# Order of the first loads and place of the bias tables in a hybrid sparse-attention decoder step

## The chip, the cores and the metric

The kernel runs on one core of a Trainium2 chip. The metric is device time in microseconds (us) of one execution. The core has five engines, each with an instruction queue of its own that is worked off in order: TensorE (PE in the profile; its weight loads are listed apart as PEld), VectorE (DVE), ScalarE (ACT), GpSimd (POOL) and SyncE (SP), which here issues nearly all DMA transfers. TensorE runs at one of two clocks, 1.2 or 2.4 GHz.

## What is computed

One layer of a decoder, for a prompt of 512 tokens and 8 sample tokens that share the weights. The part that matters here is the head of the layer: an adaLN modulation of the input by a condition vector, then the input projections. All logits of the attention branches get a bias that depends on the distance alone, from a table of 32 buckets by 16 heads.

```python
shift, scale, gate = jnp.split(jax.nn.silu(c) @ w_ada + b_ada, 3, axis=-1)
h = x * (1.0 + scale[:, None, :]) + shift[:, None, :]
parts = jnp.split(h @ w_in, np.cumsum(IN_WIDTHS)[:-1], axis=-1)
...
bias_c = tab_g[:, t5_bucket(dist_c), :].transpose(1, 0, 3, 2)
s_c = jnp.einsum('bqgrd,bngd->bqgrn', qc, ck) * scale + bias_c
```

Behind it come three attention branches (compressed, selected, window), a block-sparse branch, gates, projections and a LayerNorm. The change does not touch these.

## The kernel before

A scheduler places the instructions of each engine; the code gives dependences, priorities by the order of writing, and a few explicit orders.

The width of 1024 is cut into 8 tiles of 128 channels. For each tile `j`, `load_ada(j)` fetches two pieces of the adaLN weights (`u<-ada_ss`, 128x1024 f32 each, so 1.05 MB a tile), `load_x(j)` the tile's rows of the transposed x (128x520). `ada(j)` multiplies the weights with the condition (`s<-u,cs`, 8 matmuls into one bank of the two called `s`), ACT copies the result to `a`, two small matmuls (`s<-cst,a`) turn it into columns, DVE adds the bias (`ssh`), and ACT and DVE form h of this tile as a high and a low part (`hTh`, `hTl`). `ada(j)` also asks for the loads of tile `j + 3`. The weights of two successive tiles share one buffer `u`, and there are two such buffers: the loads of tiles 4 and 5 wait until TensorE has read tiles 0 and 1, those of 6 and 7 until it has read 2 and 3.

Three projections of h (columns `kc`, `vc`, `ks`) are worked as the tiles come: `early_load` fetches a column block of weights (`raw<-w_cols`, 128x1024) and splits it in high and low parts on ACT, DVE and POOL (`v`, `kd`, `kl`), and `early_mm(n, k)` adds tile `k` to the sums with 6 matmuls 128x260 for each of the three, 18 a tile and 144 in all, into the banks `d`, `d`, `d`, `o`, `e`, `pt`.

`tables()` makes the bias tables from two inputs, `tabx` (33x272) and `e` (33x3010), which lie in the buffer `y`: one matmul 16x384, 15 matmuls 128x8, and two of 128x194 and 128x130, each block into a bank that DVE then copies out (`bs`, `bc`, `bdn`, `bdm`). Before the change these use the one bank `e`. `bs` is written out to DRAM much later, for the attention.

Behind the last tile, TensorE goes on with the other projections (`d<-hTh,hl`), merged with the compression network and then with the attention. Their weights come through SP's queue behind the loads of the start, in the order of the code; an SP load waits, too, until the load eight places ahead of it has landed. Behind the adaLN loads stand small ones: `pt16` (from which DVE computes `vidx`) and `pos`.

Of the kernel before, what the change touches and what calls it, by code (L numbers as in the profile page):

```python
# [190 lines left out]
def build(tc, A):  # L191
    nc = tc.nc
# [4 lines left out]
    def mm(out, lhsT, rhs, start, stop):  # L197
        if glue[1] is None:
            i = mmraw(out, lhsT, rhs, start=start, stop=stop, skip_group_check=True)  # L199
        else:  # L200
            with tc.high_priority():
                i = mmraw(out, lhsT, rhs, start=start, stop=stop, skip_group_check=True)  # L202
            order(i, glue[1])
        if glue[0]:
            glue[1] = i
        return i
# [19 lines left out]
    def lo(out, x, hi, eng=None):  # L226

        if eng is None:
            eng = engs[0][turns[0] % len(engs[0])]
            turns[0] += 1  # L230
        (nc.gpsimd if eng == "p" else nc.vector).tensor_sub(out, x, f32(hi))  # L231
# [4 lines left out]
    with ExitStack() as es:  # L236
# [10 lines left out]
        def bank(tag, bufs):  # L247
            return ps.tile([128, 512], F32, name=tag, tag=tag, bufs=bufs)

        def p_d():  # L250
            return bank("d", 3)

        def p_s():
            return bank("s", 2)
# [7 lines left out]
        def p_e():  # L262
            return bank("e", 1)

        def row(tag, bufs=1):
            return kvp.tile([128, NT], F32, name=tag, tag=tag, bufs=bufs)

        def pair(tag, dtype):
            return kvp.tile([128, 2, NT], dtype, name=tag, tag=tag, bufs={"kd": 3, "v2": 2}[tag])
# [78 lines left out]
        def expect(n):  # L348
            got = next(at_w)
            assert got == n, (got, n)  # L350
# [42 lines left out]
        e, tabx = y2[:33, 0:NE], y2[:33, NE:NE + 272]  # L393
# [15 lines left out]
        def load_x(j):  # L409
            if j < 8:  # L410
                if j < 4:
                    xr[j] = row(*(("ev", 2), ("z", 1), ("tmp", 1), ("ev", 2))[j])
                else:
                    xr[j] = st.tile([128, NT], F32, name="xr", bufs=4)
                nc.sync.dma_start(xr[j], A["xT"][j])
# [6 lines left out]
        def load_ada(j):  # L422
            if j >= 8 or j in ss:
                return
            if j % 2 == 0:
                ss["t"] = u_tile(F32)
            ss[j] = ss["t"][:, j % 2]
            for hf in range(2):
                c = slice(hf * 1024, hf * 1024 + 1024)
                ss["dma"] = nc.sync.dma_start(ss[j][:, c], A["ada_ss"][j][:, c])  # L430

        def ada(j):

            p = p_s()
            for hf in range(2):
                for k in range(4):
                    c = hf * 1024 + k * 256
                    mm(p[32 * k:32 * k + 32, :256], cs[:, hf * 4 + k], ss[j][:, c:c + 256], hf == 0, hf == 1)
            load_x(j + 3)
            load_ada(j + 3)  # L440
            a = st.tile([128, 256], F32, name="a", bufs=2)
            nc.scalar.copy(a, p[:, :256])
            for i in range(2):
                D["seli"] = mm(p[:, 256 + i * 16:266 + i * 16], a[:, 128 - i * 128:256 - i * 128], const("seli"), True, True)
            nc.vector.tensor_add(ssh[:, j], view(p, 256, [[16, 2], [1, 10]]), view(bT, j, [[8, 2], [0, 10]]))
            x = xr.pop(j)
            h = st.tile([128, NT], F32, name="h")
            sh, s1 = (ssh[:, j, i] for i in range(2))
            D["act"] = nc.scalar.activation(hTh[:, j, :T], x[:, :T], AF.Identity, scale=s1[:, 0:1], bias=sh[:, 0:1])
            nc.vector.tensor_mul(h[:, T:], x[:, T:], s1[:, 1:9])  # L450
            nc.vector.tensor_add(h[:, T:], h[:, T:], sh[:, 1:9])
            nc.vector.tensor_copy(hTh[:, j, T:], h[:, T:])
            nc.vector.tensor_scalar(h[:, :T], x[:, :T], s1[:, 0:1], sh[:, 0:1], op0=OP.mult, op1=OP.add)
            D["dve"] = nc.vector.tensor_sub(hTl[:, j], h, f32(hTh[:, j]))
# [3 lines left out]
        def tables():  # L458

            nc.gpsimd.memset(bc[:, :, 0:16], 0.0)  # L460
            nc.gpsimd.memset(bc[:, :, 31:64], BIG)
            nc.gpsimd.memset(cv2, 0.0)
            nc.gpsimd.memset(zn, 0.0)
            p = p_e()
            mm(p[:16, :384], tabx[:, 0:16], e[:, E_BAND:E_CMP], True, True)
            bs = st.tile([16, 384], F32, name="bs")
            nc.vector.tensor_copy(bs, p[:16, :384])
            D["band"] = bs
            p = p_e()
            for m in range(15):  # L470
                mm(p[:, m * 8:m * 8 + 8], e[:, E_CMP + m * 128:E_CMP + m * 128 + 128], tabx[:, 0:8], True, True)
            nc.vector.tensor_copy(bc[:, :, 16:31], p[:, :120].rearrange("p (m h) -> p h m", h=8))
            p = p_e()
            mm(p[:, :194], tabx[:, 16:144], e[:, E_DEC:E_WIN], True, True)
            mm(p[:, 256:386], tabx[:, 144:272], e[:, E_DEC:E_DEC + 130], True, True)
            nc.vector.tensor_copy(bdn, p[:, :194])
            nc.vector.tensor_copy(bdm, p[:, 256:386])
# [3 lines left out]
        def early_load(n):  # L481

            expect(n)
            raw = W.take(0)
            early_w[n] = []
            for hf in range(2):
                if n == "ks" and hf:
                    t = [kvp.tile([128, T], F32R, name="kl", tag="kl", bufs=2) for _ in range(2)]
                else:
                    t = pair("v2" if n == "kc" else "kd", F32R)  # L490
                    t = [t[:, x, :512] for x in range(2)]
                nc.scalar.copy(t[0], HALVES[hf](raw))
                lo(t[1], HALVES[hf](raw), t[0])
                early_w[n].append(t)

        def early_mm(n, k):
            if k == SELI_K:
                with tc.issue_after(D["seli"].ins):
                    return early_mms(n, k)
            early_mms(n, k)  # L500
# [9 lines left out]

        EARLY = "kc", "vc", "ks"
        nc.sync.dma_start(cT, A["cT"])
        nc.sync.dma_start(tabx, A["tabx"])
        nc.sync.dma_start(e, A["e"])
        load_ada(0)
        nc.sync.dma_start(cst0, A["cst"][:, :NC0])
        nc.sync.dma_start(bT, A["bT"])
# [8 lines left out]
        for j in range(3):  # L526
            if j:
                load_ada(j)
                load_x(j)
            early_load(EARLY[j])  # L530
        for j in range(9):
            if j < 8:
                ada(j)
            if j == 1:
                tables()
            if j:
                for n in EARLY:
                    early_mm(n, j - 1)
# [1035 lines left out]
        p = p_d()  # L1574
# [4 lines left out]
        for tt in range(4):  # L1579
            next(few, None)  # L1580
            c = 0
            for n in PARTS[tt]:
                p = p_d()[:, :n]
# [111 lines left out]
```

## Time and profile before

| | |
|---|---|
| timed runs | 657.27, 663.61, 663.81 us; median 663.61 us |
| the profiled execution | 660.91 us, of which the span in the trace is 659.1 us |
| mean granted TensorE clock in it | 0.974 |
| busy: PE, DVE, ACT, POOL | 619.0 (94%), 310.5, 295.2, 287.3 us |
| DMA | 124.77 MB, mean 189 GB/s |

A row of a timeline gives the start of a group of like instructions, how long it lasts, the engine, line, operation and what is read and written (output <- inputs), the count, and in brackets how long the engine sat idle ahead of it and what ended that. The matmuls of `s<-u,cs`, `s<-cst,a` and `e<-y` count twice in the timeline, since they run in two passes (a row of x16 `s<-u,cs` is the 8 matmuls of a tile); those of 128x260 count once. The ends of matmuls are modelled, so the start of the next row tells better how long a group took. A granted clock of 1.00 stands in rows of the windows ahead of the first change of clock that was recorded, whatever the clock was.

### The profile page before, as it was taken

Reading aid. Unit: us, or ns where it says so; the run is one execution under the profiler, and the core shown is the slowest. Engines: PE = TensorE matmul, PEld = TensorE weight load, DVE = VectorE, ACT = ScalarE, POOL = GpSimd, SP = SyncE. Lnnn points to the kernel's source line nnn. Section 1 sums busy time; section 2 is a strip of 40 time slices with the busy share of each in tenths; the row PEclk is TensorE's granted clock in tenths of the full one; section 3 lists DMA queues with packets and bytes.
Section 4 is the critical chain, followed back from the end, with each engine's and each line's share of the span. In section 5 each row is a group of like instructions: output and inputs, shape, how many; then the busy total and the mean of one; then the engine's idle time right before and its main releaser. Section 6 shows DMA issues by size and latency. Waiting matters only on the chain.

```text
span 659.1 us, 13320 instructions
## 1 busy us (share of the span) xinstructions
PE 619.0 (94%) x4747; PEld 518.1 (79%) x4747; DVE 310.5 (47%) x800; ACT 295.2 (45%) x679; POOL 287.3 (44%) x328
## 2 busy tenths in 40 slices
PE   6999999999979799999999899998988999999993
PEld 4778999999959578776879679865635998999672
DVE  1465543532572664335355446744431145545177
ACT  2248455544443545444445446645433353433521
POOL 1105466542352433442364544445432264655746
PEclk9998999999998969999999989999998999999998
DMA  8895554539953594699775563168977344345102
GB/s 309 337 293 188 167 179 144 171 98 97 165 186 104 155 360 141 216 310 311 245 229 196 196 237 97 49 220 312 304 264 288 100 153 137 96 129 188 68 24 106
DMA packets 64132, 124.77 MB, mean 189 GB/s; under 512 B 8142, under 2 KB 28368, under 8 KB 63521
## 3 DMA queue, kind: packets, MB, share of 16 engines
q1 hardware_dynamic: 61954, 116.58, 52.9%
q0 software_dynamic: 2112, 7.34, 6.3%
q8 instruction: 37, 0.61, 0.4%
q14 instruction: 29, 0.24, 0.1%
HBM read 112.76 MB, written 11.13 MB: 188 GB/s over the span
## 4 chain that ended last, share of the span: by engine, by line
PE 66%; DMA 6%; SPq 3%; DVE 3%; issue 2%; ACT 1%; POOL 1%; POOLq 0%; ACTq 0%; DVEq 0%
PE d L199 40%; PE s L199 9%; PE e L199 7%; DMA raw<-mobv 3%; PE pt L1025 3%; SPq L721 2%; PE o L202 2%; PE o L199 2%; PE pt L199 1%; PE e L202 1%; DMA raw<-slcv,vidx 1%; DMA raw<-winv 1%; DVE xt L1488 1%; DMA craw<-cmp 1%; SPq L717 0%
## 5 line engine op out<-in xcount | busy, mean ns | idle before, releaser
L199 PE MATMUL d<-hTh,hl 128*128 128x260 f32 (+1 forms) x1408 | 273.1, 290 | 1.4 <-DVE hl L231 1.1
L199 PEld LDWEIGHTS d<-hTh,hl 128*128 128x128 f32 (+1 forms) x1408 | 221.4, 189 | 16.8 <-issue 9.4
L199 PE MATMUL d<-hTl,hl 128*128 128x260 f32 (+1 forms) x704 | 201.4, 287 | 0.0
L199 PEld LDWEIGHTS d<-hTl,hl 128*128 128x128 f32 (+1 forms) x704 | 133.2, 189 | 3.2 <-issue 2.5
L231 POOL TENSOR_TENSOR hl<-raw,hl 128x512 fp32r<-128x512 f32 x56 | 73.5, 1314 | 104.2 <-ACT hl L310 99.6
L310 ACT CAST hl<-raw 128x512 fp32r<-128x512 f32 (+1 forms) x111 | 67.8, 615 | 76.1 <-PE d L199 62.6
L1018 POOL TENSOR_SCALAR p<-p,sm,gp 128x512 f32<-128x512 f32 (+1 forms) x64 | 40.0, 626 | 95.8 <-DVE sm L1017 91.2
L1016 ACT ACTIVATE p<-s,sm 128x512 f32<-128x512 f32 (+1 forms) x96 | 50.8, 530 | 65.9 <-PE pt L1025 54.0
L231 DVE TENSOR_TENSOR hl<-raw,hl 128x512 fp32r<-128x512 f32 (+1 forms) x55 | 53.5, 974 | 49.4 <-ACT hl L310 47.6
L199 PE MATMUL d<-yh,hl 128*128 128x260 f32 x256 | 46.3, 282 | 0.0
L1025 PE MATMUL pt<-cst,p 128*128 128x128 f32 x240 | 40.3, 282 | 1.5 <-DVE pp L1030 0.8
L199 PEld LDWEIGHTS d<-yh,hl 128*128 128x128 f32 x256 | 39.7, 188 | 1.0 <-issue 0.4
L199 PE MATMUL s<-kd,q 128*128 128x512 f32 (+1 forms) x96 | 35.1, 366 | 4.6 <-ACT p L1016 4.6
L1010 DVE TENSOR_REDUCE sm<-s 128x1 f32<-128x256 f32 (+1 forms) x48 | 16.9, 354 | 44.9 <-PE s L199 43.9
L1025 PEld LDWEIGHTS pt<-cst,p 128*128 128x128 f32 x240 | 27.8, 142 | 11.5 <-issue 5.8
L1018 POOL TENSOR_SCALAR p<-p,sm,cst 128x512 f32<-128x512 f32 (+3 forms) x32 | 19.5, 611 | 38.1 <-DVE sm L1017 37.9
L199 PE MATMUL d<-yl,hl 128*128 128x260 f32 x128 | 36.0, 282 | 0.0
L199 PE MATMUL s<-u,w1h 128*128 128x256 f32 (+1 forms) x160 | 33.5, 301 | 1.2 <-ACT u L793 0.7
L1012 DVE CUSTOM_DVE_ANT_0 s<-s,band 128x256 f32<-128x256 f32 (+1 forms) x48 | 17.3, 362 | 35.2 <-PE s L199 24.8
L199 PEld LDWEIGHTS s<-kd,q 128*128 128x128 f32 x96 | 18.6, 194 | 17.8 <-ACT p L1016 8.6
L231 POOL TENSOR_TENSOR u<-craw,u 128x512 fp32r<-128x512 f32 x16 | 21.3, 1331 | 24.8 <-ACT u L828 24.8
L199 PE MATMUL s<-kd,qx 128*128 128x512 f32 (+1 forms) x96 | 31.5, 330 | 0.0
(425 smaller groups left out, 1167.3 us busy)
## 6 DMA issues: line engine op xcount, KB each, us to landing
raw<-w_cols SPq DMA_DIRECT2D x46, 512.0 KB
raw<-mobk SPq DMA_DIRECT2D x64, 256.0 KB
raw<-mobv SPq DMA_DIRECT2D x64, 256.0 KB
u<-ada_ss SPq DMA_DIRECT2D x16, 512.0 KB
craw<-cmp SPq DMA_DIRECT2D x64, 128.0 KB
raw<-slck SPq DMA_DIRECT2D x64, 64.0 KB
raw<-ada_g SPq DMA_DIRECT2D x8, 512.0 KB
raw<-w_up SPq DMA_DIRECT2D x8, 512.0 KB
```

Of the source, the lines that this page charges most:

```text
L199: i = mmraw(out, lhsT, rhs, start=start, stop=stop, skip_group_check=True)
L202: i = mmraw(out, lhsT, rhs, start=start, stop=stop, skip_group_check=True)
L231: (nc.gpsimd if eng == "p" else nc.vector).tensor_sub(out, x, f32(hi))
L310: nc.scalar.copy(h, src)
L721: dyn.append(nc.sync.dma_start(out, A[name][bass.ds(page, 1)].rearrange("a p c -> p (a c)")))
L1010: nc.vector.tensor_reduce(sm[:, 0:1], s[:, :b], axis=AX, op=OP.min)
L1012: nc.vector.tensor_tensor_reduce(out=s[:, b:n], in0=s[:, b:n], in1=j.band[:, 256 - (n - b):], scale=1.0, scalar=top, op0=OP.add, op1=OP.mi ...
L1016: nc.scalar.activation(pr, s[:, :n], AF.Exp, scale=-1.0, bias=sm[:, 1:2], accum_out=sm[:, 2:3])
L1018: nc.gpsimd.tensor_scalar(pr, pr, sm[:, 3:4], j.gate(i), op0=OP.mult, op1=OP.mult)
L1025: nc.tensor.transpose(p[:, k * 128:k * 128 + 128], j.p[i][:, kb * 128:kb * 128 + 128], ident)
L1488: add(xt[tt][:, c], xt[tt][:, c], u)
```

## The change

The loads of `tabx` and `e` are issued behind those of adaLN tile 1 and its rows of x, and no longer ahead of tile 0. `tables()` is written behind `ada(3)`, and no longer behind `ada(1)`. Its three blocks take a bank of the pair `s`, which the adaLN tiles use as well, in place of the bank `e`.

```diff
-            p = p_e()
+            p = p_s()
             mm(p[:16, :384], tabx[:, 0:16], e[:, E_BAND:E_CMP], True, True)
...
-            p = p_e()
+            p = p_s()
             for m in range(15):
...
-            p = p_e()
+            p = p_s()
             mm(p[:, :194], tabx[:, 16:144], e[:, E_DEC:E_WIN], True, True)
...
         nc.sync.dma_start(cT, A["cT"])
-        nc.sync.dma_start(tabx, A["tabx"])
-        nc.sync.dma_start(e, A["e"])
         load_ada(0)
...
             if j:
                 load_ada(j)
                 load_x(j)
+            if j == 1:
+                nc.sync.dma_start(tabx, A["tabx"])
+                nc.sync.dma_start(e, A["e"])
             early_load(EARLY[j])
         for j in range(9):
             if j < 8:
                 ada(j)
-            if j == 1:
+            if j == 3:
                 tables()
```

TensorE's queue from its first matmul on, before. The tables are `e<-y`, the adaLN tiles 0 and 1 `s<-u,cs`:

```order
L199 MATMUL e<-y 16x384
L199 MATMUL s<-u,cs 32x256 x4
L199 MATMUL e<-y 128x8 x10
L199 MATMUL s<-u,cs 32x256 x4
L199 MATMUL e<-y 128x8 x5
L199 MATMUL s<-u,cs 32x256 x8
L199 MATMUL s<-cst_72,a 128x10 x2
L199 MATMUL e<-y 128x194
L199 MATMUL e<-y 128x130
L199 MATMUL s<-cst_72,a 128x10 x2
L199 MATMUL s<-u,cs 32x256 x8
L199 MATMUL d<-hTh,v_136 128x260 x4
```

The same place after; `v` holds the weights of `kc`, `kd` here those of `vc`:

```order
L199 MATMUL s<-u,cs 32x256 x8
L199 MATMUL s<-cst_72,a 128x10 x2
L199 MATMUL s<-u,cs 32x256 x4
L199 MATMUL d<-hTh,v_134 128x260 x4
L199 MATMUL d<-hTl,v_134 128x260 x2
L199 MATMUL s<-u,cs 32x256 x4
L199 MATMUL s<-cst_72,a 128x10 x2
L199 MATMUL d<-hTh,kd 128x260
L199 MATMUL o<-hTh,kd 128x260
L199 MATMUL s<-u,cs 32x256 x4
L199 MATMUL d<-hTh,kd 128x260
```

The tables are gone from here, and the first early projections stand between the halves of adaLN tile 1 and ahead of tile 2, where before they stood behind tile 2.

The place in TensorE's queue to which the tables went (`s<-y`), after; ahead of its first row stand the second half of adaLN tile 3 and the columns of tile 2, and the row of `s<-cst` here is the columns of tile 3:

```order
L199 MATMUL s<-y 16x384
L199 MATMUL d<-hTh,v_134 128x260 x2
L199 MATMUL d<-hTh,kd 128x260 x2
L199 MATMUL e<-hTh,kd 128x260 x2
L199 MATMUL d<-hTh,v_134 128x260 x2
L199 MATMUL o<-hTh,kd 128x260 x2
L199 MATMUL pt<-hTh,kd 128x260 x2
L199 MATMUL s<-cst_72,a 128x10 x2
L199 MATMUL s<-y 128x8 x15
L199 MATMUL s<-y 128x194
L199 MATMUL s<-y 128x130
L199 MATMUL d<-hTl,v_134 128x260 x2
```

All of the tables now stand behind adaLN tile 3, in the midst of the early projections for tile 2.

VectorE's queue behind the tables' first copy, after; `h<-xr` is tile 4's h:

```order
L472 COPY bc<-s 128x8x15
L476 COPY bdn<-s 128x194
L477 COPY bdm<-s 128x130
L445 TENSOR_TENSOR ssh<-s,bT 128x20
L543 TENSOR_SCALAR vidx<-pt_107,cst_72 128x8
L450 TENSOR_TENSOR h<-xr,ssh 128x8
L453 TENSOR_SCALAR h<-xr,ssh 128x512
```

`vidx`, which needs the load of `pt16`, stands ahead of the h of tile 4 here; before, it stood behind that of tile 5.

## Rows read from the trace of the kernel before

**Rows 1.** The page: the chain that ended last, shares of the span by engine.

```profile
PE 66%; DMA 6%; SPq 3%; DVE 3%; issue 2%; ACT 1%; POOL 1%; POOLq 0%; ACTq 0%; DVEq 0%
```

**Rows 2.** Timeline of TensorE, 6.5 to 24 us: start, length, what, idle time ahead.

```profile
6.54 1.44 PE L199 MATMUL e<-y 33*16 33x384 f32 x2 [6.54 <-DMA y<-e]
7.91 1.08 PE L199 MATMUL s<-u,cs 128*32 128x256 f32 x8
8.92 4.43 PE L199 MATMUL e<-y 33*128 33x8 f32 x20
13.28 1.08 PE L199 MATMUL s<-u,cs 128*32 128x256 f32 x8
14.29 2.30 PE L199 MATMUL e<-y 33*128 33x8 f32 x10
16.52 1.93 PE L199 MATMUL s<-u,cs 128*32 128x256 f32 x16
18.39 1.03 PE L199 MATMUL s<-cst,a 128*128 128x10 f32 x4
19.34 1.44 PE L199 MATMUL e<-y 33*128 33x194 f32 x4
20.72 1.02 PE L199 MATMUL s<-cst,a 128*128 128x10 f32 x4
21.67 1.93 PE L199 MATMUL s<-u,cs 128*32 128x256 f32 x16
23.53 1.24 PE L199 MATMUL d<-hTh,v 128*128 128x260 f32 x4
```

**Rows 3.** The same timeline from 24 us to the end of the start.

```profile
24.57 0.64 PE L199 MATMUL d<-hTh,kd 128*128 128x260 f32 x2
25.00 0.64 PE L199 MATMUL o<-hTh,kd 128*128 128x260 f32 x2
...
27.82 0.33 PE L199 MATMUL pt<-hTh,kd 128*128 128x260 f32 x1
27.98 0.40 PE L199 MATMUL d<-hTl,v 128*128 128x260 f32 x2
...
30.43 1.07 PE L199 MATMUL s<-u,cs 128*32 128x256 f32 x16
...
34.45 0.51 PE L199 MATMUL s<-cst,a 128*128 128x10 f32 x4
34.89 1.50 PE L199 MATMUL s<-u,cs 128*32 128x256 f32 x24
...
40.89 0.40 PE L199 MATMUL d<-hTh,kd 128*128 128x260 f32 x2
41.13 0.41 PE L199 MATMUL e<-hTh,kl 128*128 128x260 f32 x2
...
52.37 0.51 PE L199 MATMUL d<-hTh,hl 128*128 128x260 f32 x2
```

**Rows 4.** DMA view of 0 to 70 us: GB/s in 40 slices of 1.75 us.

```profile
GB/s 0 120 268 329 360 417 409 408 419 405 415 420 398 394 403 413 389 68 75 323 344 300 303 139 283 194 358 398 332 337 257 168 307 171 0 0 157 205 254 150
```

**Rows 5.** Timeline of ScalarE: splits of the first two weight blocks, and `pos`.

```profile
11.01 1.14 ACT L492 CAST v<-raw 128x512 fp32r<-128x512 f32 x2 [8.14 <-DMA raw<-w_cols]
...
15.48 1.14 ACT L492 CAST kd<-raw 128x512 fp32r<-128x512 f32 x2 [0.68 <-DMA raw<-w_cols]
...
41.27 0.21 ACT L784 CAST u<-pos 128x16 fp32r<-128x16 f32 x1 [0.16 <-DMA pos<-pos]
```

**Rows 6.** Timeline of TensorE at 60 us: narrow matmuls of the compression network.

```profile
60.38 0.39 PE L199 MATMUL s<-u,w1h 128*128 128x66 f32 x2
...
61.95 0.36 PE L199 MATMUL s<-u,w1h 128*128 128x66 f32 x1 [0.68 <-ACT u L793]
```

**Rows 7.** Windows of 1 us: us, busy of PE, PEld, DVE, ACT, POOL, granted clock, DMA.

```profile
61.00:62.00 1.00, 0.32 (x3) 0.08 (x2) 0.72 (x2) 0.96 (x3) 0.23 (x1) 1.00 0.00 0
62.00:63.00 1.00, 1.00 (x6) 0.91 (x6) 0.93 (x4) 0.98 (x3) 0.00 (x0) 0.52 0.00 0
...
65.00:66.00 1.00, 1.00 (x9) 0.86 (x7) 0.00 (x0) 0.00 (x0) 0.52 (x1) 0.77 0.83 234
```

## The prediction

> **What bounds the kernel now.** The page's chain of waits comes first: matmuls on TensorE make up two thirds of it, and DMA 6% [rows 1]. Nothing in the body waits for a fixed time; transfers run at 189 GB/s in the mean, where the start shows over 400 [rows 4]. So what the start takes less, the end takes less, and the edit is judged by one number: when TensorE turns from the early projections to the first `d<-hTh,hl`, before at 52.37 us [rows 3].
>
> TensorE's own timeline comes next. It starts at 6.54, when `e` has landed, and from there on its rows follow each other almost without a hole up to 52.37 [rows 2, 3]. That it is the bound of the start, and not the loads, is seen at adaLN tile 2: TensorE comes to it at 21.67, and its 5.28 MB of loads had passed by 17.0 (below).
>
> The second thing to see there is the clock. Rows of 128x260 start 0.43 us apart for two at 24.57 and 25.00, which is 0.215 us each; at 40.89 and 41.13 it is 0.24 for two, 0.12 each [rows 3]. The first is what 260 columns take at 1.2 GHz, the second is 2.4 GHz. The short ones begin between 27.82 and 27.98. So 21.4 us of the start, from 6.54 to 27.9, ran at half speed, and all of the tables lie in it: 1.37 + 4.36 + 2.23 + 1.38 = 9.34 us from each table row's start to that of the next [rows 2].
>
> **The loads.** Summing the slices of the DMA view [rows 4] gives the MB that had passed by each time. The first weight block, at 2.39 MB in SP's order, is reached at 10.0 and ScalarE starts on it at 11.01; the second, at 4.23 MB, is reached at 14.4 and started at 15.48 [rows 5]. A load is thus usable 1.0 us behind its place on the curve. The edit takes the 0.43 MB of `tabx` and `e` from ahead of tile 0. Tile 0 then stands at 1.09 in place of 1.52 MB, usable at 7.5 instead of 8.7 us; tile 1 at 3.00 in place of 3.44 MB, 12.5 instead of 13.5. The tables now stand ahead of the second weight block, so that it and all behind it keep their places: 15.4 us for that block, 16.7 and 18.0 for the halves of tile 2, 19.9 for the third block, 23.1 for tile 3. That alone is about 1 us for two tiles that TensorE reached late anyway. The gain must come from TensorE.
>
> **TensorE's queue, step by step at 1.2 GHz.** Prices: half an adaLN tile 0.93 (1.86 from 21.67 to 23.53), its columns 0.95 (18.39 to 19.34), a 128x260 0.215 [rows 2, 3]. Tile 0 ends at 8.5, its columns at 9.9, and its h is there at about 12, since ScalarE splits the first weight block first. Tile 1's first half runs at 11.2, six matmuls of `kc` from 12.1, tile 1's second half and columns until 15.9. Two matmuls of `vc` follow when its block is split, then tile 2's first half, landed at 16.7, until 17.7. From 17.7 on every row has its input: sixteen 128x260, tile 2's second half, then `ks`. So the unbroken run of 128x260 that began at 23.53 before begins at 17.7, and tile 3 is read at about 25 instead of 30.43. That also closes the hole in the transfers (68 and 75 GB/s in the slices from 29.75 to 33.25 [rows 4]): the loads of tiles 6 and 7 wait for the buffer that tile 3 frees, and at 25 some 5 us of loads are still queued. With 10.4 MB passed by 29.75 and 2.2 MB left at 400 GB/s, tile 7 is usable at 36.3.
>
> **When the clock rises.** Before, the short rows begin 4.4 us behind the start of that run (23.53 to 27.9). I move the rise along with the run, to 22.1. Bounds: moved along with the first six matmuls of `kc` at 12.1, it is 16.5; not moved at all, 27.9.
>
> The Trainium skill (TensorE: Matmul & The Clock Gate, Part 1) says that the low clock is the default and that activity releases it. By that the tables could be a warm-up that the edit takes away, and the time would move to the late-rise rival below. The trace does not agree that they warm it: 10 us of tables and adaLN tiles from 6.54 on left the rows at 24.57 long [rows 2, 3].
>
> **The sum.** At 27.95 before, 24.4 us were left to 52.37. At the rise after, there is left the same, plus the tables, less four 128x260 (24 early ones done by 22.1 instead of 20): 0.5. The tables at 2.4 GHz are not in the trace. Their 30 passes of 128x8 are nearest to the columns of 128x10: 0.44 us for four at 34.45 [rows 3], so 3.3 us; the wide ones, 2.75 at 1.2 GHz, shrink as 0.215 to 0.12, to 1.5. I take 4.8, with 4.7 (half) and 9.3 (no gain) as bounds. That makes 24.4 + 4.8 - 0.5 = 28.7, and an end at 22.1 + 28.7 = 50.8: **1.6 us less**. The bank pair costs little: the 15 matmuls wait for VectorE to read tile 3's columns, and tile 4 for the copy of `bc`, but 128x260 rows stand between. Against the profiled 660.91 this is 659.3 us. The median of the runs shown is 663.61, 2.7 above the profiled one, and they spread from 657.27 to 663.81; I keep to the profile and let the range hold the spread.
>
> **Rivals.**
> *The loads become the bound.* If the clock rises near 16.5, TensorE catches up with tile 3, usable at 23.1. Behind that stand 0.5 of tile 3, 4.8 of tables, 108 matmuls (13.0), four tiles (4.1), six column pairs (2.6), and about 1.4 of small holes as before: end at 49.5, 2.9 less, 658.0 us. This is the most that the edit can bring. Against it: the short waits up to 17.7.
>
> *The tables pull the clock down.* They now run in the fast stretch, 4 us of narrow matmuls in a row. For it: behind 2.6 us of matmuls of 66 columns and a hole of 0.68 us the granted clock stood at 0.52 in the window from 62, and was back at 65.5 [rows 6, 7]. Against: there a hole and transposes came between. Such a fall is 3.5 us at half speed, 1.75 us of work: the gain is gone, 661.1.
>
> *The clock rises as late as before* (the other side). The early projections now stand among the adaLN rows, and the start has more waits. Each us of delay costs half: at 27.9 the end is 50.8 + 2.9 = 53.7, 1.3 later than before, 662.2. It decides at 25.3. Against: from 17.7 the rows are those that stood ahead of the rise before.
>
> *`vidx` holds VectorE.* It now stands ahead of tile 4's h and needs a small load from behind tile 7. Before, `pos`, beside it, landed at 41.27 [rows 5]. After, it should land at about 37, and VectorE comes to it at 38 (50.8 less 12.6 of work behind it). If the hole in the transfers stayed, it would be 41.3 + 12.6 = 53.9, or 662.4. It decides at 39.8.
>
> **How the numbers follow.** Forecast 0.52; loads as bound 0.18; tables pull the clock down 0.13; late rise 0.12; `vidx` 0.05. All lie between 658.0 and 662.4, within 1% (6.6 us, about what a measurement of this kernel can tell from no change) of 660.91. The range adds the spread of the runs, about 3 us to either side, less the outer tenth: 655.5 to 663.5. Since the runs alone spread by 1%, I leave 0.12 for faster, most of it from the first two cases, and 0.05 for slower, from the last two.
>
> **What would show it.** Right: no `e<-y` at the start, the first 128x260 near 12, 0.12 us spacing from about 22, tile 3 read at 25, no slices under 100 GB/s before 36, the tables in about 4.8 us near 28, and `d<-hTh,hl` at 50.8. Wrong: 0.215 us spacing at 26; a granted clock of 0.5 behind the tables; VectorE waiting for `pt16`; or a start shorter by 2 us with no shorter span, which would mean that the body, not TensorE, sets the end.

## The result and the profile after

The changed kernel is slower: 664.88 us in the median of 22 runs (659.63 to 668.72) against 661.38 for the kernel before in 22 runs beside them. The ratio is 1.0068, with a 95% interval of 1.0046 to 1.0091. That is within the 1% that the prediction calls "same", but above its range (655.5 to 663.5), and it went the other way: 3.5 us more, where 1.6 less was forecast.

| | before | after |
|---|---|---|
| profiled execution, its span | 660.91, 659.1 us | 661.58, 659.8 us |
| first early projection | 23.53 | 12.29 |
| 128x260 rows 0.12 us apart from | 27.9 | 21.7 |
| first `d<-hTh,hl` (end of the start) | 52.37 | 55.60 |

The two profiled executions happen to lie only 0.7 us apart; single executions of either kernel scatter by 9 to 13 us, so the span can't judge 3 us. (The profiles of e1, e6, e9 and e16 below are of executions over 1.5% above their kernel's fastest, so no comparison of times rests on one of them alone.) The last line of the table can, as the experiments show: the same kernel run again gave 52.03 for before.

TensorE's timeline of the changed kernel, which answers to [rows 2, 3] (start, length, what, idle time ahead):

```profile
5.47 2.30 PE L199 MATMUL s<-u,cs 128*32 128x256 f32 x16 [5.47 <-DMA u<-ada_ss]
8.26 1.03 PE L199 MATMUL s<-cst,a 128*128 128x10 f32 x4 [0.49 <-ACT a L442]
...
12.29 1.24 PE L199 MATMUL d<-hTh,v 128*128 128x260 f32 x4
...
15.46 0.61 PE L199 MATMUL s<-cst,a 128*128 128x10 f32 x4 [0.49 <-ACT a L442]
18.10 0.48 PE L199 MATMUL d<-hTh,kd 128*128 128x260 f32 x1 [2.03 <-ACT kd L492]
...
21.30 0.57 PE L199 MATMUL d<-hTh,kd 128*128 128x260 f32 x2
21.71 0.41 PE L199 MATMUL d<-hTh,v 128*128 128x260 f32 x2
21.95 0.40 PE L199 MATMUL o<-hTh,kd 128*128 128x260 f32 x2
...
24.95 0.64 PE L199 MATMUL s<-u,cs 128*32 128x256 f32 x8
...
26.64 0.81 PE L199 MATMUL s<-y 33*16 33x384 f32 x2
27.38 0.51 PE L199 MATMUL d<-hTh,v 128*128 128x260 f32 x2
...
29.36 5.55 PE L199 MATMUL s<-y 33*128 33x8 f32 x34
34.84 0.80 PE L199 MATMUL d<-hTl,v 128*128 128x260 f32 x2
35.44 0.42 PE L199 MATMUL d<-hTl,kd 128*128 128x260 f32 x1
35.65 0.42 PE L199 MATMUL o<-hTl,kd 128*128 128x260 f32 x1
...
55.60 0.51 PE L199 MATMUL d<-hTh,hl 128*128 128x260 f32 x2
```

Up to 26.64 it goes roughly as forecast, but for the 2.03 us of idle time ahead of 18.10 and for one thing more: the clock was up once already. The adaLN columns took 1.03 us at 8.26 and 0.61 at 15.46, so by then TensorE ran at 2.4 GHz. Behind the idle time the clock fell (0.63 in the window from 18), and the rows from 18.82 to 21.3 are long again: a first fall of 3.4 us. Then comes the tables' block, 30 passes of the narrow matmuls and 4 of the wide ones (29.36 to 34.84). Behind it the single 128x260 rows stand 0.21 us apart again (35.44, 35.65), where they had been at 0.12 since 21.71 (0.24 for two). The windows show the same as a granted clock (third column from the right; then the DMA share and GB/s):

```profile
18.00:19.00 1.00, 0.87 (x6) 0.60 (x10) 0.92 (x2) 1.00 (x3) 0.35 (x1) 0.63 0.99 391
...
30.00:31.00 1.00, 1.00 (x11) 1.00 (x10) 0.86 (x4) 0.56 (x1) 0.00 (x0) 1.00 1.03 414
31.00:32.00 1.00, 1.00 (x11) 1.00 (x10) 0.46 (x1) 0.00 (x0) 0.00 (x0) 0.95 1.03 410
32.00:33.00 1.00, 1.00 (x6) 1.00 (x7) 0.00 (x0) 0.00 (x0) 0.00 (x0) 0.50 1.03 410
...
36.00:38.00 2.00, 2.00 (x11) 2.00 (x10) 0.00 (x0) 0.00 (x0) 0.00 (x0) 0.50 0.66 220
38.00:39.00 1.00, 1.00 (x9) 0.74 (x11) 0.00 (x0) 0.00 (x0) 0.00 (x0) 0.63 0.14 39
39.00:40.00 1.00, 1.00 (x17) 0.46 (x10) 0.00 (x0) 0.00 (x1) 0.00 (x0) 1.00 0.42 70
```

TensorE was busy without a hole, and yet its clock fell to 1.2 GHz some 2.5 us into the block, at about 31.9. It came back at 38.7: a window at 0.95 counts for 0.1 us at half speed, one at 0.63 for 0.74, so 0.1 + 6 + 0.74 = 6.84 us, which cost 3.4 us of work.

The loads, as [rows 4] (40 slices of 1.75 us) and [rows 5]:

```profile
GB/s 0 180 344 369 344 297 420 298 241 375 403 412 415 398 388 413 400 419 407 404 296 144 78 336 230 386 405 138 267 337 9 9 157 194 290 120 0 26 133 231
```

```profile
17.43 1.14 ACT L492 CAST kd<-raw 128x512 fp32r<-128x512 f32 x2 [2.02 <-DMA raw<-w_cols]
```

The second weight block is split at 17.43 instead of 15.48, behind two slices of 298 and 241 GB/s (12.25 to 15.75) where before 408 and 419 stood. The queues were not idle there. In the window from 14 the DMA share is 1.02 at 241 GB/s, where other windows with that share move over 400. The kernel before has such a window too, but early, while it loads `tabx` and `e` (the second row):

```profile
14.00:15.00 1.00, 0.97 (x8) 0.09 (x8) 0.00 (x0) 0.00 (x0) 0.00 (x0) 1.00 1.02 241
5.00:6.00 1.00, 0.00 (x0) 0.00 (x0) 0.00 (x0) 0.00 (x0) 0.00 (x0) 1.00 0.94 242
```

So the slow stretch moved together with the two loads.

The page's chain (as [rows 1]) has less of TensorE in it and more DMA:

```profile
PE 59%; DMA 11%; SPq 4%; DVE 3%; issue 2%; ACT 1%; POOL 0%; POOLq 0%; ACTq 0%; DVEq 0%
```

That shows no new wait by itself. Half of the DMA share is the write of `bs` to DRAM, issued at 150.3 us and landing 36.4 later; before, it was issued at 146.9 and took 36.5. What the pair of numbers tells is that the start's lateness, 3.2 us at its end, is handed on as far as that (3.4 us here).

### The profile page after: what moved, and what is told of

Its sections match the earlier page's. It is cut to its first block, busy times and chain, and to the rows that moved or that the text cites. A ratio compares the mean times of both kernels' runs of the same rounds, so it can differ in the third digit from the quotient of the medians.

```text
span 659.8 us, 13319 instructions
## 1 busy us (share of the span) xinstructions
PE 614.9 (93%) x4747; PEld 512.9 (78%) x4747; DVE 312.6 (47%) x800; ACT 294.8 (45%) x679; POOL 287.7 (44%) x328
## 4 chain that ended last, share of the span: by engine, by line
PE 59%; DMA 11%; SPq 4%; DVE 3%; issue 2%; ACT 1%; POOL 0%; POOLq 0%; ACTq 0%; DVEq 0%
PE d L199 34%; PE s L199 8%; PE e L199 6%; DMA band_d<-bs 6%; SPq L722 4%; PE pt L1026 3%; PE o L202 3%; DMA raw<-mobv 2%; PE o L199 2%; PE pt L199 1%; PE e L202 1%; DMA ew<-tabx 1%; DMA raw<-slcv,vidx 1%; DMA raw<-winv 1%; DVE xt L1489 1%
## 5 line engine op out<-in xcount | busy, mean ns | idle before, releaser
L199 PEld LDWEIGHTS d<-hTh,hl 128*128 128x128 f32 (+1 forms) x1408 | 219.5, 188 | 19.6 <-issue 10.2
L231 DVE TENSOR_TENSOR hl<-raw,hl 128x512 fp32r<-128x512 f32 (+1 forms) x55 | 50.9, 925 | 54.8 <-ACT hl L310 52.9
```

## The experiments

The theory under test: the tables, put into the fast stretch, pull the clock down, and the shift of the start's end reaches the end of the program. The rivals: the loads, whose new order delays the second weight block, or the tables' mere place. This table gathers all runs by the end of the start in their profile; "low" is the time at 1.2 GHz behind the first rise of the clock and ahead of that end, from the windows. In the change and in e12, 3.4 and 6.8 us of it lie ahead of tile 3, behind idle time of TensorE.

| run | end of start, us | low, us | ratio to before (95%) |
|---|---|---|---|
| e13 one pass, tables where they were | 49.47 | 0 | 1.0025 (0.9982 to 1.0069) |
| e16 the same again | 49.60 | 0 | 1.0020 (0.9974 to 1.0065) |
| e15 before again | 52.03 | 0 | 1.0012 (0.9968 to 1.0056) |
| e14 tables moved, one pass | 52.49 | 3.4 | 1.0039 (1.0000 to 1.0077) |
| e11 before, dense matmuls ahead | 53.18 | 17.1 | 1.0044 (1.0007 to 1.0081) |
| e3 after without narrow ones | 54.13 | 3.4 | 1.0147 (1.0112 to 1.0181) |
| e12 after, one pass | 54.35 | 10.2 | 1.0045 (0.9997 to 1.0092) |
| the change | 55.60 | 10.2 | 1.0068 (1.0046 to 1.0091) |
| e2 tables moved alone | 55.77 | 6.8 | 1.0099 (1.0058 to 1.0139) |
| e6 tables behind tile 7 | 55.99 | 3.4 | 1.0245 (1.0173 to 1.0316) |
| e0 the change again | 56.93 | 6.8 | 1.0062 (1.0027 to 1.0098) |
| e4 loads moved alone | 57.63 | 0 | 1.0072 (1.0024 to 1.0120) |
| e5 narrow ones in three blocks | 59.06 | 6.8 | 1.0084 (1.0054 to 1.0115) |
| e8 before, 256 columns | 61.22 | 3.4 | 1.0165 (1.0137 to 1.0194) |
| e10 narrow ones braided in | 61.98 | 17.1 | 1.0123 (1.0083 to 1.0164) |
| e7 after, 256 columns | 62.32 | 13.7 | 1.0193 (1.0153 to 1.0233) |
| e1 loads moved alone, bank `e` | 63.50 | 23.9 | 1.0157 (1.0109 to 1.0204) |
| e9 dense ones between | 65.55 | 17.1 | 1.0151 (1.0089 to 1.0213) |

TensorE's order behind the start is that of the changed kernel or of before in all but e3 and e6, whose order the scheduler changed in dozens of places further on; their ratios tell nothing.

**The change again (e0).** No edit.

> The changed kernel once more, unchanged, beside the others of this call. Expected 0.4 to 0.9% over the kernel before. Theory A (the tables let the clock fall): the granted clock is at 0.5 for 6 to 7 us from about 32 us on, and d<-hTh,hl starts at 55 to 56. If instead the clock falls elsewhere or not at all in this execution, and the start still ends at 55 or later, theory A is wrong about the place.

The ratio agrees, and the fall at the tables is as long (34.2 to 41.0 us, 3.5 us into the block). But the end of the start came 1.3 us later than in the first profile, a little past the expected 55 to 56. In this execution the clock was not up early: the columns at 15.83 still took the 1.03 us of the slow clock, and it rose at about 23.9, not at 21.7.

```profile
15.83 1.03 PE L199 MATMUL s<-cst,a 128*128 128x10 f32 x4 [0.49 <-ACT a L442]
```

**Tables alone (e2), loads alone (e4, e1).** e2 has the loads as before and the tables as after. e4 is the changed kernel with the tables put back behind tile 1; e1 is the same in the bank `e`.

```diff
 e2, against after
+        nc.sync.dma_start(tabx, A["tabx"])
+        nc.sync.dma_start(e, A["e"])
         load_ada(0)
...
-            if j == 1:
-                nc.sync.dma_start(tabx, A["tabx"])
-                nc.sync.dma_start(e, A["e"])
 e4, against after
-            if j == 3:
+            if j == 1:
                 tables()
```

> The loads of tabx and e first, as in the kernel before; tables behind adaLN tile 3 and in the bank pair, as in the changed kernel. Theory A: the tables still stand in the fast stretch, so the clock falls at 31 to 33 and is low for 6 to 7 us; the second weight block is 2 us earlier than in the changed kernel (15.5 for 17.4), so d<-hTh,hl starts at 54 to 55. Theory C (the place of the loads costs, not that of the tables): 52 or earlier.

> The loads in the order of the changed kernel, the tables left behind adaLN tile 1 in their own bank e as before. Theory A: the tables run at the low clock among waits, as before, and nothing falls later; tables land later and hold up the dense rows, so the rise is not much earlier than 27.9: d<-hTh,hl at 51 to 53, time level with before (within 1 us). Theory C (the new order of the loads itself is what costs, by pushing the second weight block back by 2 us): d<-hTh,hl at 55 or later, 3 us slower than before.

> The changed kernel's loads and banks, with the tables put back behind tile 1, so that they run in the stretch at 1.2 GHz. Theory A: no fall of the clock from 24 us on once it has risen; the tables wait for the late table load (usable about 14 us) and take about 9 us at the lower clock, the rise comes at 28 to 32 us, the start ends at 53 to 56 us. Rival, bank sharing made the earlier run of late loads with early tables slow (63.5 us), and here the tables are free of it: 52 to 53 us. If that run's low clock until 41 us came from narrow products standing among the dense ones, the start ends past 60 us again whichever bank they use.

e2 has the whole loss: its start ends 3.40 us after that of before (the change: 3.23), and its windows show the same fall, beginning 2.6 us behind the narrow ones' start at 30.01 (0.64 in a window is 1.44 us at half speed):

```profile
30.00:32.00 2.00, 2.00 (x22) 2.00 (x18) 0.00 (x0) 0.37 (x1) 0.00 (x0) 1.00 0.40 121
32.00:34.00 2.00, 2.00 (x13) 1.95 (x12) 0.00 (x0) 0.00 (x0) 0.00 (x0) 0.64 0.95 336
34.00:36.00 2.00, 2.00 (x9) 2.00 (x10) 1.79 (x7) 0.82 (x1) 0.00 (x0) 0.50 0.99 320
```

The loads have a price of their own. In e4 TensorE first waits for `e`, then works the tables at the low clock, and the dense run that lifts the clock begins behind them (rise at about 31.2 instead of 27.9); no fall follows:

```profile
15.85 1.44 PE L199 MATMUL s<-y 33*16 33x384 f32 x2 [1.01 <-DMA y<-e]
...
18.81 7.85 PE L199 MATMUL s<-y 33*128 33x8 f32 x34
```

The start's end, 57.63, met none of the three expectations (53 to 56, 52 to 53, past 60). In e1 the clock stood at 0.5 from 18.0 to 41.9, with the tables among the dense rows until 33.5; e4, with the tables in the bank `s`, has no such stretch. What kept it low in e1 beyond 33.5 is not shown. So neither half of the edit is worth anything by itself.

**Without the narrow ones (e3).** The 15 matmuls and their copy give way to a memset.

```diff
-            for m in range(15):
-                mm(p[:, m * 8:m * 8 + 8], ...)
-            nc.vector.tensor_copy(bc[:, :, 16:31], ...)
+            nc.gpsimd.memset(bc[:, :, 16:31], 0.0)
```

> The changed kernel without the 15 narrow matmuls and the copy behind them (that part of the bias table is set to zero instead, which is left out of the computation). Theory A: the clock does not fall; what goes is the 4.9 us of these rows at the low clock and about 1.9 us of half speed behind them: d<-hTh,hl at about 49. Theory B: only the work itself goes, and the rows behind still run 0.215 us apart for some us: 51.

The clock did not fall where it does in after:

```profile
30.00:36.00 6.00, 6.00 (x55) 4.34 (x54) 2.13 (x8) 1.19 (x2) 0.00 (x0) 1.00 1.02 402
36.00:42.00 6.00, 5.81 (x64) 4.20 (x61) 3.15 (x12) 2.37 (x5) 0.00 (x0) 1.00 0.66 201
```

The loads and the three wide table matmuls are as in after, so it is the narrow ones that pull it down there. The start ended at 54.13, past both expectations (49 and 51): the changed order brought 2.60 us of idle time, and there the clock fell after all, with no narrow matmul near: behind it two dense rows took 0.43 us, not 0.24.

```profile
51.36 0.80 PE L199 MATMUL d<-hTh,v 128*128 128x260 f32 x2 [2.60 <-DVE hTh L452]
51.96 0.64 PE L199 MATMUL o<-hTh,kd 128*128 128x260 f32 x2
52.39 0.64 PE L199 MATMUL pt<-hTh,kl 128*128 128x260 f32 x2
```

Without the two, some 1.7 us for the clock and 2.6 for the wait, it would have ended near 49.8; that is an estimate.

**Other places for the narrow ones (e5, e6, e9, e10).** Three blocks of five behind tiles 4, 5 and 6; all behind tile 7; a dense 128x260 behind each; or each behind one of the 18 early projections of tile 3.

```diff
 e5
-            for m in range(15): ...
+            if 4 <= j <= 6:
+                narrow(j - 4)
 e6
-            if j == 3:
+            if j == 7:
                 tables()
 e9
                 mm(p[:, m * 8:m * 8 + 8], ...)
+                mm(p[:, 128:388], hTh[:, 0, 0:128], hTh[:, 0, 0:260], True, True)
 e10
+                            if m < 15:
+                                mm(p[:, m * 8:m * 8 + 8], ...)
```

> The changed kernel with the 15 narrow matmuls in three blocks of 5, one behind each of adaLN tiles 4, 5 and 6, each with a bank and a copy of its own; all of the work stays, and early projections stand between the blocks. Theory A: no block is long enough to let the clock fall; the granted clock stays at 1.0 from 22 to 50 us and d<-hTh,hl starts at 52 to 53, some 3 us before the changed kernel's 55.60, time 2 to 4 us under the changed kernel. Theory B (the shared banks and the order cost, not the clock): two more banks taken from the adaLN tiles make it worse, 56 or later.

> The changed kernel with tables() written behind adaLN tile 7, so that no table stands between the tiles. Theory A: the clock stays up until tile 7, tile 7's columns come about 8 us earlier than in the changed kernel, and the fall comes with the tables at about 45, where some 6 us run at half speed: d<-hTh,hl at 54 to 56, no better than the changed kernel. If the fall does not come there, 51 to 52, and the place between the tiles was the trouble.

> The changed kernel with one more matmul of 128x260 behind each of the 15 narrow ones (h of tile 0 with itself, into columns of the same bank that nothing reads): 15 x 0.12 = 1.8 us of work added, place, banks and the order of everything else as in the changed kernel. Theory A: the clock does not fall; tables from 29.4 to 35.3 us (3.3 + 0.7 + 1.8), no row 0.215 us apart behind them, d<-hTh,hl at about 54.0 in place of 55.60 in spite of the added work. Theory B (banks and order cost, the clock is a bystander): the added work comes on top, 57 or later.

> The changed kernel with the 15 narrow matmuls braided, one by one, into the 18 early projections of adaLN tile 3, so that the dense rows between them are work that has to be done anyway. Theory A: the granted clock stays at 1.0 between 22 and 60 us; d<-hTh,hl at 52 to 52.5, level with the kernel before (52.37), time 3 us under the changed kernel and within 1 us of the kernel before. Theory B: 55 to 56 as in the changed kernel.

Every one of them fell. e5 falls in its second block of five, 0.9 us behind the start of that block at 39.64; its first and third block, of the same size, draw no fall. From 24 to 30.7 us its rows lie within 0.05 us of e0's, and its low time is the same, yet its start ends 2.1 us later (59.06 against 56.93): the fall does not account for that part. e6 falls at 52.5, 4.5 us behind the start of its narrow ones at 47.99: the fall goes with the tables, not with the time. e9 and e10, which were to keep the clock up by dense neighbours, have the longest falls at the tables, 17.1 us each (33.2 to 50.3 and 34.5 to 51.6). e10's rows show what interleaving does: one pair of narrow passes and one dense matmul take 0.63 us before the fall and 1.04 behind it, so a dense matmul that costs 0.12 among its like costs some 0.3 beside a narrow one.

```profile
33.33 0.39 PE L202 MATMUL d<-hTh,v 128*128 128x260 f32 x1
33.65 0.39 PE L202 MATMUL s<-y 33*128 33x8 f32 x2
33.96 0.39 PE L202 MATMUL d<-hTh,v 128*128 128x260 f32 x1
...
34.59 0.59 PE L202 MATMUL d<-hTl,v 128*128 128x260 f32 x1
35.11 0.59 PE L202 MATMUL s<-y 33*128 33x8 f32 x2
35.63 0.59 PE L202 MATMUL d<-hTh,kd 128*128 128x260 f32 x1
```

**Wider ones (e7, e8).** The narrow matmuls with 256 columns instead of 8, in after and in before.

```diff
-                mm(p[:, m * 8:m * 8 + 8], e[...], tabx[:, 0:8], True, True)
+                mm(p[:, m * 8:m * 8 + 256], e[...], tabx[:, 0:256], True, True)
```

> The changed kernel, but the 15 narrow matmuls of the tables take 256 columns of tabx in place of 8 (the surplus columns are written over or not read), so that each keeps its place and its count while the array works through it. Theory A (the narrow matmuls in the fast stretch let the clock fall): the rows of 128x260 behind the tables stay 0.12 us apart, the 15 take about 3.3 us, and d<-hTh,hl starts at 52 instead of 55.60; the time is some 3 us under the changed kernel, about level with the kernel before. Theory B (the tables cost what they cost by their place, the shared bank pair and the order around them): d<-hTh,hl at 55 or later, no gain.

> The kernel before, with the same widening: 256 columns in place of 8 in the 15 matmuls at the start, where they run at 1.2 GHz and take 0.22 us either way. Theory A: wide matmuls lift the clock where narrow ones do not, so the short rows begin well ahead of 27.9 us (at 11 to 18), and d<-hTh,hl starts at 47 to 50 instead of 52.37, 3 us or more off the time. Theory B (the clock depends only on TensorE being busy at all): no change, 52.4.

Wide f32 passes over 33 rows do not hold the clock either: in e7 it falls at 32.2, 3.1 us into the block, and stays low to 45.8. They did not lift it either: in e8 TensorE worked without idle time from 6.46 on, and the clock rose at about 32, behind the first dense rows at 31.28. Their price was put too low; 20 passes took 8.90 us at 1.2 GHz, 0.44 each.

**Dense matmuls ahead of the tables of before (e11).** 31 matmuls of 128x260 on zeros into the idle bank `pt`, 16 before the first tile and one behind each narrow one in the code.

```diff
+        warm(16)
         for j in range(9):
...
                 mm(p[:, m * 8:m * 8 + 8], ...)
+                warm(1)
```

> The kernel before with 31 matmuls of 128x260 on zeros at its start, into the bank pt that is idle there; 28 of them stand ahead of the first table, where TensorE waits for its first load until 6.54. They test whether dense rows alone, with no load to wait for, raise the clock early, and whether the tables then lower it again. Theory A: rows come 0.12 us apart well ahead of 27.9; the 13 narrow matmuls in a row lower the clock once, at 10 to 15, as they do in the changed kernel; d<-hTh,hl at 49 to 52. If the tables did not lower it, 47 to 48, where the loads of the last tiles end.

The scheduler put 28 of them in one run at the front, and that makes the run a good test in the place where the tables always stood:

```profile
1.93 5.31 PE L199 MATMUL pt<-hTl 128*128 128x260 f32 x28 [1.93 <-DVE hTl L516]
7.17 0.81 PE L199 MATMUL e<-y 33*16 33x384 f32 x2
7.91 0.63 PE L199 MATMUL pt<-hTl 128*128 128x260 f32 x3
```

The clock was up by 7.17: the 33x384 row takes 0.74 us to the next start, where it took 1.37 in [rows 2]. Then the narrow ones began at 9.87, and 2.7 us later it was gone, until 29.6; the start ended at 53.18, past the expected 49 to 52:

```profile
10.00:12.00 2.00, 2.00 (x19) 2.00 (x20) 0.44 (x1) 1.09 (x3) 0.00 (x0) 1.00 1.01 408
12.00:13.00 1.00, 1.00 (x9) 1.00 (x8) 0.26 (x1) 0.32 (x2) 0.87 (x1) 0.78 1.04 406
13.00:14.00 1.00, 1.00 (x3) 0.22 (x3) 0.00 (x0) 0.00 (x0) 0.39 (x1) 0.50 1.04 417
```

**A shorter block (e12, e14, e13).** The operands of the narrow ones are cast to the rounded type of the projections, so that each runs in one pass instead of two: e12 in after, e14 in e2, e13 in before. The order behind the start stays.

```diff
+                nc.scalar.copy(hTl[:33, 4, 512:520], tabx[:, 0:8])
+                for m in range(4):
+                    w = 512 if m < 3 else 384
+                    nc.scalar.copy(hTl[:33, 4 + m, :w], e[:, E_CMP + m * 512:E_CMP + m * 512 + w])
...
-                mm(p[:, m * 8:m * 8 + 8], e[...], tabx[:, 0:8], True, True)
+                mm(p[:, m * 8:m * 8 + 8], hTl[:33, 4 + m // 4, ...], hTl[:33, 4, 512:520], True, True)
```

> The changed kernel with the 15 narrow table products in one pass instead of two: ScalarE casts their two operands to the rounded type behind the table load, 5 casts of at most 33x512. The block shrinks from 30 records (4.2 us in the 2.4 GHz stretch of the changed kernel) to 15, an estimated 2.1 us. Theory A, the tables pull the clock down, which fell 2.5 us into the block: the block is out before that, no 2-us window between 24 and 48 us is under 0.95, and the first d<-hTh,hl starts at 55.6 - 3.3 (time lost at the lower clock) - 2.1 = about 50.2 us, 2 us before that of the kernel before; ratio 0.995 to 1.000. Rival, the fall comes from where the tables stand and not from how long they run: windows of 0.50 between 30 and 42 us again, start over at 53.5 us, ratio about 1.004. Rival, the late second weight block is what costs: the start ends at 53 us or later with no fall.

> The loads as before, the tables moved behind tile 3, and the 15 narrow products in one pass as in the run before this one. With two passes this version's start ended at 55.77 us with a fall of the clock from 32.7 to 39.3. Theory A: no fall, 55.77 - 3.3 - 2.1 = 50.4 us, ratio 0.995 to 1.000, no later than the version with late loads. Rival (place, not length): fall between 30 and 42 us again, 53.7 us, ratio about 1.005.

> The kernel before with the 15 narrow products in one pass, nothing else moved. At 1.2 GHz the block falls to half its time, some 3.2 us less of the slow stretch. If TensorE's own work is the bound of the start, the first d<-hTh,hl starts at about 52.4 - 3.2 = 49.2 us and the ratio is about 0.995; if the loads are the bound (the third weight block was usable at 19 to 20 us), at 51 to 52.4 us with idle rows of up to 3 us before 24 us, ratio 0.998 to 1.002. Either way no fall of the clock before 60 us.

The narrow ones shrank from 3.3 us (at 2.4 GHz, see below) to 1.7, and the fall at the tables from 6.8 to 3.4 us, but it did not go away. e14:

```profile
30.36 1.83 PE L199 MATMUL s<-hTl 33*128 33x8 f32 x15
32.12 0.61 PE L199 MATMUL s<-cst,a 128*128 128x10 f32 x4
32.67 0.81 PE L199 MATMUL s<-y 33*128 33x194 f32 x4
33.41 1.91 PE L199 MATMUL s<-u,cs 128*32 128x256 f32 x16
```

```profile
32.00:34.00 2.00, 2.00 (x18) 1.62 (x21) 1.37 (x7) 0.81 (x1) 0.00 (x0) 0.87 0.99 346
34.00:36.00 2.00, 2.00 (x19) 0.98 (x10) 1.03 (x3) 0.37 (x1) 0.00 (x0) 0.50 0.91 287
36.00:38.00 2.00, 2.00 (x15) 2.00 (x14) 0.00 (x0) 0.00 (x0) 0.00 (x0) 0.77 0.91 337
```

Behind its one-pass block, columns, wide tables and an adaLN tile follow at once, and the fall comes 3.1 us behind the block's start. The expectation of no fall missed; that the length matters and not the place alone held in these two pairs. Length alone does not set the fall, though: e5's block of ten passes drew 6.8 us. Against e2 the start of e14 ends 3.3 us earlier (52.49), of which about 1.7 us are work less lost to the half clock and 1.6 us fewer narrow passes; the clock also rose 0.9 us later in e14 (19.8 against 18.9), so the sum is not exact. e12 ends at 54.35, since its casts stand ahead of a column copy that tile 1 waits for: 3.60 us of idle time, and a fall of 6.8 us behind it. e13's start ends 2.9 us ahead of that of before.

**Does the end of the start carry (e15, e16).** Before and e13, again.

> The kernel before, unchanged: how far the start of one profiled execution stands for the others. If the start repeats, the first d<-hTh,hl is within 1 us of 52.37 and the clock is not under 0.95 in a 2-us window between 28 and 60 us. Ratio 1.000 within 0.003.

> The kernel before with one-pass narrow products, again, with more rounds. Its start ended 2.9 us earlier than that of before, and its time was level. If the lead carries through, the ratio is 0.9956 and the first run's level time was scatter; if the program gives it back behind the start, the ratio is 0.998 to 1.003 with the first d<-hTh,hl at 49 to 50 us again, and the two traces of this call show at which microsecond the lead is lost.

```profile
52.03 0.51 PE L199 MATMUL d<-hTh,hl 128*128 128x260 f32 x2
```

```profile
49.60 0.51 PE L199 MATMUL d<-hTh,hl 128*128 128x260 f32 x2
```

The first row is e15's, the second e16's; both starts repeat within 0.4 us. Later ends go with longer times: from 52 to 62 us the ratio climbs from 1.001 to 1.012 and more, 0.8 to 1.3 us for each us of lateness in the eight of them whose start ends over 4 us late, with the order behind it unchanged. The match is not close: e14 ends the start level with before, and its ratio is 1.0039 with an interval from 1.0000. An earlier end does not show: e13 and e16 lead by 2.4 to 2.9 us, which would be 0.9956 to 0.9964, and both intervals begin above that. In the profile of e13 the lead of 2.9 us is still there at the end (6.8 us, in an execution of 654.08), so no wait that swallows it was seen there; what costs the other executions their lead stays open. No version here beats the kernel before.

## Why the prediction was wrong, step by step

**What bounds the kernel.** Right so far as the milestone goes: TensorE bounded the start, and its lateness of 3.2 us came back as 3.5 in the medians. The other half of the premise, that what the start takes less the end takes less, is not shown: the shorter starts of e13 and e16 gave ratios of 1.0025 and 1.0020.

**The loads: wrong.** "All behind it keep their places" failed. The second weight block was split at 17.43, not 15.4; by the slices its 4.23 MB had passed at 15.2, not 14.4, and it came 2.2 us behind its place on the curve, not 1.0. With the loads as before and the tables moved (e2) the block was split at 15.44, so it is `tabx` and `e` in their new place that held it up. The forecast took the curve of the loads for one of time alone, where its slow slices belong to these two transfers and moved with them (241 GB/s at a DMA share of 1.02). That speaks for the transfers of 33 rows and against the order in SP's queue; no run separates the two. It left TensorE idle for 2.03 us, and at the rise 16 early projections and half of tile 2 were done, where I had 24 and the whole tile by 22.1: 8 x 0.12 + 0.57 = 1.5 us.

**The rise: right, in part by luck.** 21.7 against 22.1, and tile 3 was read at 24.95 as forecast. But the first rise came by 15.46, nearer to the bound of 16.5 than to the 22.1, and it was lost again behind the idle time; 21.7 is the second. In e0 there was one rise, at 23.9, and tile 3 was read at 26.29. The late-rise rival, which decides at 25.3, is out in both.

**The tables' price: right.** 33x384 took 0.74 us; the block took 5.48, of which 2.9 at half speed, so 4.03 at 2.4 GHz: 4.77 in all against 4.8. Without the wide ones, 0.75 at that clock, the narrow ones are the 3.3 that were priced.

**The sum: its clock failed.** This is the step that decided the miss. It took 2.4 GHz for all that stands behind the rise, and so put the tables at 4.8 us with no fall behind them. Of 33.9 us from 21.7 to 55.6, 5.2 are above the 28.7 of the sum: 3.4 for the fall, 1.5 for what was undone at the rise, and 0.3 that I do not place. The rival "tables pull the clock down" named the mechanism and had 0.13. Its size was too small: one fall like that of [rows 7], 3.5 us, where this block drew 6.8. Its evidence against, that a hole and transposes stood behind the earlier fall, did not hold: here PE had neither, and the clock fell all the same. The forecast's error was to let the narrow matmuls of 128x10 in [rows 3] set the price of the tables with the clock held at 2.4 GHz; four or eight passes between dense rows did, 30 did not.

**The tables as a warm-up.** The Trainium skill (TensorE: Matmul & The Clock Gate, Part 1) says that activity releases the low clock. In e11 the trace agrees for dense rows: behind 28 matmuls of 128x260 the clock was up by 7.17 us. For the tables it does not: in e11 the clock fell again 2.7 us after the narrow ones began.

**Loads as bound, and `vidx`: out.** The slices stay above 290 GB/s from 15.75 to 36.75, and no slice below 100 comes before 38.5, as forecast; VectorE did not wait for `vidx`.

**The chances.** 0.05 for the slow side was too little. Three of my cases ended within 2 us above before, and I added none in which two of them hold at once, though a late block and a falling clock each came without the other: e2 has the fall with the block in its old place, e4 the late loads with no fall.

## What to carry to other kernels

Before moving a block of small matmuls into a fast stretch, ask what its passes do to the clock there: in the slow stretch it cost its own time, in the fast one also half of the microseconds that follow at 1.2 GHz. Look for a run of like matmuls elsewhere in the trace and read the granted clock behind it, and if there is a fall, put it into the sum with a wide range; here the falls at such blocks lasted from 3.4 to 17.1 us. And read what stands behind a load that is moved back: it takes the place of something.

## What the runs showed of the hardware

- A busy TensorE can lose its clock. With no hole between rows, matmuls over 33 rows brought it from 2.4 to 1.2 GHz, mostly 2.5 to 3.5 us after their block began (after, e2, e11, e7, e14, e0), with 8 columns or 256, and in one pass as in two. Two falls lie outside that: 4.5 us in e6, and 0.9 us into the second block of e5. Without the narrow ones it held at that place (e3). Which of their properties does it was not separated.
- The clock also fell beside idle time of TensorE: behind 2.03 us in the changed kernel (0.63 in the window from 18), and with 2.60 us in e3 (0.43 us from one pair of dense rows to the next at 51.96).
- The fall lasted 3.4 us with 1.7 us of narrow passes, 6.8 with 3.3, 13.7 with wide ones that took some 11, and 17.1 when the narrow ones were braided with dense ones (e14, after, e7, e10). Braiding made it worse here.
- Dense matmuls on zeros lifted the clock (e11, up by 7.17), while it was still low at 31 us behind 256-column f32 passes on 33 rows (e8).
- The full DMA share does not mean full speed: 241 GB/s at a share of 1.02 in the window from 14 us of the changed kernel, against 414 at 1.03 in that from 30.
